# Thirteen seven-product pairs per layer in place of eleven, and a third weight sum made by an accumulating DMA

## The chip, the cores and the metric

The kernel runs on one core of one Trainium2 chip. The metric is the device time of one execution in microseconds (us), taken as the median of several runs. The engines are TensorE (PE, with its weight loads as PEld), VectorE (DVE), ScalarE (ACT), GpSimd (POOL) and SyncE (SP); POOL and SP here mostly issue transfers to the DMA engines.

## The reference, cut to what matters

The model has two layers over 512 tokens of width 1024, all in float32. Each layer has four token mixers and then a gated feed-forward part (FFN) of width 2816 with a causal convolution of three taps. The change touches the FFN's first projection alone:

```python
hf = rms_norm(x, norm_ffn_pre[l])
u = causal_depthwise_conv(hf @ ffn_w_up[l], ffn_conv_w[l], ffn_conv_b[l])
gate, val = jnp.split(u, 2, axis=-1)
f = (jax.nn.gelu(gate, approximate=True) * val) @ ffn_w_down[l]
x = x + rms_norm(f, norm_ffn_post[l])
```

## The kernel before

A float32 product is made of three matmuls of a faster type: each operand is split into a high part (`whi`, a copy by ACT) and the rest (`wlo`, a subtraction by DVE), and high by high, high by low and low by high are summed in PSUM (`mm`, L306). The normalized tokens stand in `hT_hi` and `hT_lo`.

The 2 × 2816 columns of the projection are 22 pairs of 128 gate columns and 128 value columns. Pairs 0 and 1 come in `head`, the others in the loop at the end of the FFN code, in one of two ways. A **plain** pair is two calls of `proj`, 48 matmuls of 512 columns into the tiles `ps`. A pair in the set `SEVEN` (L81) is a **seven pair**: its 2 × 2 block product (two halves of the inner dimension, gate and value columns by two halves of the tokens) is made from seven block products in place of eight, by sums of token blocks (t1 to t4, made once per layer and half by `forms`) and sums of weight blocks (s1 to s4). Its 84 matmuls have 256 columns each and go into the tiles `sa`, `sb` and `se`.

`seven(i)` issues its products in this order: (0,0), then d4 of the pair before; (1,0); d2, whose weights are s2; then (1,1) of the pair before, whose weights are s4; d1 with s1; d3 with s3. All of (0,0), d2, d3 and d4 accumulate in the same bank `sa`, so between them ACT copies partial sums out: L1410 after (0,0), L1418 after d2, L1424 after d3. A copy must be done before the next product adds into the bank.

The weights of a seven pair come as follows. SP loads the first half of the inner dimension as one tile `raw` of 128x1024 (L177), and three slots `rs` of 128x512: L170 (to be s1), L171 (to be s3) and L172 (a block as it is). POOL then adds to two of them by accumulating DMAs: L173 (s1) and L174 (s3). DVE makes s2 from s1 and the first half of `raw` (L206) and s4 from s2 and its other half (L207), and `halves` splits all of them into `whi` and `wlo` (L188, L189). For a plain pair the splits are L245 and L246.

There are three `raw` tiles, four tiles each of `whi` and `wlo`, and 60 slots of 128x512 (`rs`, `s2`, `s4`, `fu` and others). SP's order of instructions is the order in which the code is written, since `MANUAL` holds SP; PE's order in the FFN is written by hand too. The order of ACT, DVE and POOL is set by a scheduler before the program runs; each engine then goes through its instructions in that order, and waits where one of them must wait.

Of the kernel before, what the change touches and what calls it, by code (L numbers as in the profile page):

```python
# [12 lines left out]
ALU = mybir.AluOpType  # L13
# [8 lines left out]
NP_ = DFF // 128  # L22
# [14 lines left out]
def unit_width(k):  # L37
    if k[0] == "fs" and k[2] >= 2:
        return 0
    return {"vt": 816, "w2": 640, "pw": 512, "up": 512}.get(k[0], 1024)  # L40
# [37 lines left out]
SLACK2 = 1.5  # L78
MAXB = 1.5

SEVEN = {i for i in range(5, NP_ - 1) if i % 3 != 1}  # L81

H_2 = 1.0
H_T = 3.0
# [21 lines left out]
def build(tc, x, wts, prm, gains, cst, out, order=None):  # L106
# [4 lines left out]
    V, A, G, T, SP = nc.vector, nc.scalar, nc.gpsimd, nc.tensor, nc.sync  # L111
    with ExitStack() as ctx:
# [10 lines left out]
        def nm(s):  # L123
            uid[0] += 1
            return f"{s}{uid[0]}"

        def slot(w=512, dt=F32, name="g"):
            return pg.tile([128, w], dt, tag="g", bufs=NG, name=nm(name))
# [10 lines left out]
        def dram(src, offset, ap):  # L139
            return src if recording else bass.AP(tensor=src.tensor, offset=src.offset + offset, ap=ap)  # L140
# [8 lines left out]
        raw, parts = {}, {}  # L149
# [9 lines left out]
        def w_dma():  # L159
            while pos["dma"] < len(order) and sum(not isinstance(r, list) for r in raw.values()) < NRAW:  # L160
                i = pos["dma"]
                w = unit_width(order[i][1])
                key = order[i][1]
                if key[0] == "fs" and key[2] == 1:
                    raw[i] = [slot(name="rs") for _ in range(3)]
                    a22, s1, s3 = raw[i]
                    blk = lambda j, c: dram(wts, offs[j] + c, [[1024, 128], [1, 512]])
                    j = i - 1
                    assert order[j][1] == ("fs", key[1], 0)
                    SP.dma_start(s1, blk(i, 512))  # L170
                    SP.dma_start(s3, blk(j, 0))  # L171
                    SP.dma_start(a22, blk(i, 512))  # L172
                    G.dma_start(s1, blk(i, 0), accum_op=ALU.add)  # L173
                    G.dma_start(s3, blk(i, 0), accum_op=ALU.add)  # L174
                elif i not in raw and w:
                    raw[i] = pw.tile([128, WMAX], F32, tag="raw", bufs=NRAW, name=nm("raw"))
                    SP.dma_start(raw[i][:, :w], dram(wts, offs[i], [[w, 128], [1, w]]))  # L177
                pos["dma"] += 1
# [3 lines left out]
        def halves(i, *srcs):  # L182

            hi = pw.tile([128, WMAX], F32R, tag="whi", bufs=NSPL, name=nm("whi"))
            lo = pw.tile([128, WMAX], F32R, tag="wlo", bufs=NSPL, name=nm("wlo"))
            c = 0
            for s, n in srcs:
                A.activation(hi[:, c:c + n], s, AF.Copy)  # L188
                V.tensor_tensor(lo[:, c:c + n], s, f(hi[:, c:c + n]), op=ALU.subtract)  # L189
                c += n  # L190
            parts[i] = (hi, lo)

        def w_seven(i):

            _, p, n = order[i][1]
            if n == 0:
                halves(i, (raw[i], 1024))
                sums[p] = [raw[i], i]  # L200
            elif n == 1:
                r1 = sums[p][0]
                raw.pop(sums[p][1])
                a22, s1, s3 = raw.pop(i)
                s2, s4 = slot(name="s2"), slot(name="s4")
                V.tensor_tensor(s2, s1, r1[:, 0:512], op=ALU.add)  # L206
                V.tensor_tensor(s4, s2, r1[:, 512:1024], op=ALU.add)  # L207
                halves(i, (s2, 512), (s1, 512))
                sums[p] = [s3, a22, s4]
            elif n == 2:  # L210
                halves(i, (sums[p][0], 512), (sums[p][1], 512))
            else:
                halves(i, (sums.pop(p)[2], 512))

        def w_split(q, roomy=False):
# [3 lines left out]
            while pos["spl"] <= min(q, len(order) - 1):  # L219
                i = pos["spl"]  # L220
                w_dma()
                w = unit_width(order[i][1])
                if order[i][1][0] == "fs":
                    w_seven(i)
                    pos["spl"] += 1
                    w_dma()
                    continue
# [12 lines left out]
                else:  # L240
# [6 lines left out]
                    parts[i] = (hi, lo)  # L247
                pos["spl"] += 1
                w_dma()

        def w_ahead(n=NSPL - 1):
# [357 lines left out]
        for l in range(L):  # L609
# [745 lines left out]
            def forms(h):  # L1355
                def block(t, k, q):
                    return f(t[:, k * 4 + h * 2:k * 4 + h * 2 + 2, q * 256:q * 256 + 256])
                hi, lo = (lambda k, q: block(hT_hi, k, q)), (lambda k, q: block(hT_lo, k, q))
                sub, add = ALU.subtract, ALU.add
                a, b = slot(name="ta"), slot(name="tb")  # L1360
                V.tensor_tensor(v2(a), hi(0, 0), hi(0, 1), op=sub)
                V.tensor_tensor(v2(b), lo(0, 0), lo(0, 1), op=sub)
                V.tensor_tensor(a, a, b, op=add)
                form["d1"].append(hilo(a, name="t1"))
                V.scalar_tensor_tensor(v2(b), v2(a), -1.0, hi(1, 1), op0=ALU.mult, op1=sub)
                V.tensor_tensor(v2(b), v2(b), lo(1, 1), op=sub)
                form["d2"].append(hilo(b, name="t2"))
                c = slot(name="tc")
                V.scalar_tensor_tensor(v2(c), v2(b), -1.0, hi(0, 0), op0=ALU.mult, op1=sub)
                V.tensor_tensor(v2(c), v2(c), lo(0, 0), op=sub)  # L1370
                form["d3"].append(hilo(c, name="t3"))
                d = slot(name="td")
                V.scalar_tensor_tensor(v2(d), v2(b), -1.0, hi(1, 0), op0=ALU.mult, op1=sub)
                V.tensor_tensor(v2(d), v2(d), lo(1, 0), op=sub)
                form["d4"].append(hilo(d, name="t4"))
# [24 lines left out]
            def seven(i):  # L1400

                ba, bb, be = bank("sa"), bank("sb"), bank("se")
                sa, sb = slot(name="ca"), slot(name="cb")
                L_, R_ = slice(0, 256), slice(256, 512)
                w0 = w_get(l, ("fs", i, 0))
                w_ahead(1)
                product(ba, w0, 0, (0, 0), True)
                A.activation(sa[:, L_], ba[:, L_], AF.Copy)  # L1410
                w_ahead(2)
                more()
                product(bb, w0, 512, (1, 0), True)
                V.tensor_tensor(bb[:, L_], bb[:, L_], sa[:, L_], op=ALU.add)
                w1 = w_get(l, ("fs", i, 1))
                w_ahead(2)
                product(ba, w1, 0, "d2", False)
                A.activation(sa[:, R_], ba[:, L_], AF.Copy)  # L1418
                w_ahead()
                more()  # L1420
                product(be, w1, 512, "d1", True)
                w2 = w_get(l, ("fs", i, 2))
                product(ba, w2, 0, "d3", False)
                A.activation(sb[:, L_], ba[:, L_], AF.Copy)  # L1424
                w_ahead()

                def four():
                    product(ba, w2, 512, "d4", False)
                    V.tensor_tensor(ba[:, R_], be[:, L_], sb[:, L_], op=ALU.add)

                def three():
                    w3 = w_get(l, ("fs", i, 3))
                    product(be, w3, 0, (1, 1), False)
                    V.tensor_tensor(bb[:, R_], be[:, L_], sa[:, R_], op=ALU.add)
                    ffn_pair(i, [bb, ba], -1.0)
                rest.extend((four, three))

            forms(0)
            for i in range(2, NP_):
                if i == 3:  # L1440
                    forms(1)
                if i in SEVEN:
                    seven(i)
# [147 lines left out]
```

## Time and profile before

| | us |
|---|---|
| median of 3 runs | 1893.99 (1893.16 to 1894.71) |
| the profiled execution | 1895.84 |
| its span from first to last instruction | 1894.1 |
| PE busy | 1873.2 (99%) |
| DVE busy | 1411.3 (75%) |
| ACT busy | 964.0 (51%) |
| POOL busy | 177.2 (9%) |

Busy times are sums over the span of the profiled execution; issuing a DMA isn't counted as busy. The granted clock of TensorE is 1.00 throughout. The FFN pairs of layer 0 lie between about 596 and 820 us, those of layer 1 in the last quarter of the span.

### The profile page before, as it was taken

To read this page: it belongs to the slowest core of one execution; us is meant where nothing else is said; L and a number is where in the kernel's file an instruction comes from. 1 tells how busy PE (TensorE), PEld (TensorE's weight loads), DVE (VectorE), ACT (ScalarE), POOL (GpSimd) and SP (SyncE) were. 2 spreads that over 40 slices of the span, in tenths; PEclk is the share of its full clock that TensorE was granted. 3 is DMA by queue.
4 is the path that set the end of the run, shared out by engine and by line. 5 is a ranking of instruction groups with operands and counts; after the bars stand their busy time and mean duration, and the time that the engine had idled before them with its cause. 6 is when DMAs were issued, how large, how long until landed. Compare 5 with 4: busy or idle time off the path is not lost.

```text
span 1894.1 us, 27567 instructions
## 1 busy us (share of the span) xinstructions
PE 1873.2 (99%) x10164; PEld 1614.9 (85%) x10164; DVE 1411.3 (75%) x2610; ACT 964.0 (51%) x1850; POOL 177.2 (9%) x313
## 2 busy tenths in 40 slices
PE   7999999999999999999999999999999999999998
PEld 7988888888888899988898888888888898999887
DVE  6898879888547888783468887897985478888722
ACT  5547576732435555562345665766224345555521
POOL 0403300000001010100023033000000010110000
PEclk9999999999999999999999999999999999999999
DMA  8523321223245365543454243112232453554332
GB/s 295 153 90 99 104 60 51 67 89 95 86 127 196 105 180 137 147 126 124 159 197 141 67 106 106 57 50 79 89 95 90 146 196 110 156 162 119 122 115 89
DMA packets 87367, 226.41 MB, mean 120 GB/s; under 512 B 12480, under 2 KB 12864, under 8 KB 87232
## 3 DMA queue, kind: packets, MB, share of 16 engines
q1 hardware_dynamic: 73728, 198.42, 32.5%
q0 software_dynamic: 13504, 26.23, 6.9%
q8 instruction: 80, 1.31, 0.3%
q14 instruction: 55, 0.45, 0.1%
HBM read 201.53 MB, written 8.39 MB: 111 GB/s over the span
## 4 chain that ended last, share of the span: by engine, by line
PE 94%; DVE 2%; issue 1%; ACT 1%; DMA 1%; POOL 0%; SPq 0%; DVEq 0%; POOLq 0%; ACTq 0%
PE ps L306 51%; PE tk L306 16%; PE sa L306 6%; PE hd L306 5%; PE o L306 3%; PE se L306 3%; PE vt L306 2%; PE sb L306 2%; PE sB L306 1%; PE sA L306 1%; PE tr L395 1%; PE tB L1086 1%; PE tA L1086 1%; PE cmp L306 1%; PE tA L1185 0%
## 5 line engine op out<-in xcount | busy, mean ns | idle before, releaser
L245 ACT ACTIVATE whi<-raw 128x1024 fp32r<-128x1024 f32 (+2 forms) x274 | 259.0, 949 | 477.7 <-PE ps L306 260.7
L246 DVE TENSOR_TENSOR wlo<-raw,whi 128x1024 fp32r<-128x1024 f32 (+2 forms) x274 | 295.9, 1084 | 232.1 <-ACT whi L245 230.5
L306 PE MATMUL ps<-hT_hi,whi 128*128 128x512 f32 x1136 | 450.2, 396 | 0.8 <-DVE ob L1105 0.8
L306 PE MATMUL ps<-hT_hi,wlo 128*128 128x512 f32 x1136 | 447.7, 394 | 0.0
L306 PE MATMUL ps<-hT_lo,whi 128*128 128x512 f32 x1136 | 446.1, 393 | 0.0
L306 PEld LDWEIGHTS ps<-hT_hi,wlo 128*128 128x128 f32 x1136 | 213.6, 188 | 47.9
L306 PEld LDWEIGHTS ps<-hT_hi,whi 128*128 128x128 f32 x1136 | 213.9, 188 | 44.8 <-DVE ob L1105 1.7
L306 PEld LDWEIGHTS ps<-hT_lo,whi 128*128 128x128 f32 x1136 | 213.9, 188 | 43.9
L908 DVE SCALAR_TENSOR_TENSOR acc<-ct,prm,acc 128x511 f32<-128x511 f32 (+14 forms) x240 | 175.6, 732 | 3.4
L306 PE MATMUL tk<-whi,fh 128*128 128x512 f32 x336 | 130.9, 390 | 0.0
L306 PE MATMUL tk<-wlo,fh 128*128 128x512 f32 x336 | 130.7, 389 | 0.0
L306 PE MATMUL tk<-whi,fl 128*128 128x512 f32 x336 | 130.7, 389 | 0.0
L1065 ACT ACTIVATE P<-P,sm 128x256 f32<-128x256 f32 (+3 forms) x128 | 70.6, 554 | 29.8 <-DVE sm L1063 28.0
L361 POOL TENSOR_TENSOR sm<-sm,mhalf 128x1 f32<-128x1 f32 x32 | 22.1, 690 | 573.1 <-DVE sm L360 573.1
L306 PEld LDWEIGHTS tk<-whi,fl 128*128 128x128 f32 x336 | 63.1, 188 | 13.2
L306 PEld LDWEIGHTS tk<-wlo,fh 128*128 128x128 f32 x336 | 63.1, 188 | 13.0
L306 PEld LDWEIGHTS tk<-whi,fh 128*128 128x128 f32 x336 | 63.1, 188 | 13.0
L306 PE MATMUL hd<-hT_hi,bh 128*128 128x256 f32 x256 | 63.4, 285 | 0.0
L306 PE MATMUL hd<-hT_hi,bl 128*128 128x256 f32 x256 | 62.4, 282 | 0.0
L188 ACT ACTIVATE whi<-rs 128x512 fp32r<-128x512 f32 x66 | 39.2, 627 | 37.5 <-PE ps L306 20.6
L1041 ACT ACTIVATE P<-P,sm 128x512 f32<-128x512 f32 (+1 forms) x80 | 47.2, 629 | 12.6 <-DVE sm L1073 9.7
L189 DVE TENSOR_TENSOR wlo<-rs,whi 128x512 fp32r<-128x512 f32 x66 | 44.3, 684 | 10.7 <-ACT whi L188 10.4
(356 smaller groups left out, 4303.4 us busy)
## 6 DMA issues: line engine op xcount, KB each, us to landing
raw<-wts SPq DMA_DIRECT2D x238, 512.0 KB, 3.5
raw<-wts SPq DMA_DIRECT2D x66, 256.0 KB, 2.6
rs<-wts SPq DMA_DIRECT2D x66, 256.0 KB, 5.2
rs<-wts POOLq DMA_DIRECT2D x44, 256.0 KB, 5.6
br<-wts SPq DMA_DIRECT2D x40, 256.0 KB, 6.1
xr<-x SPq DMA_DIRECT2D x16, 256.0 KB, 5.1
gain<-gains SPq DMA_DIRECT2D x16, 256.0 KB, 5.6
Q<-hlh POOLq DMA_DIRECT2D x64, 64.0 KB, 2.9
```

Source lines behind the costliest of these rows:

```text
L188: A.activation(hi[:, c:c + n], s, AF.Copy)
L189: V.tensor_tensor(lo[:, c:c + n], s, f(hi[:, c:c + n]), op=ALU.subtract)
L245: A.activation(hi[:, c:c + n], s, AF.Copy)
L246: V.tensor_tensor(lo[:, c:c + n], s, f(hi[:, c:c + n]), op=ALU.subtract)
L306: T.matmul(o, lhsT=lhsT, rhs=rhs, start=start, stop=stop, **kw)
L361: G.tensor_tensor(v[:, 1:2], v[:, 0:1], mhalf[:, 0:1], op=ALU.pow)
L395: T.transpose(bs[t, h][:, k * 128:k * 128 + 128], y[h][:, k * 128:k * 128 + 128], ident)
L908: V.scalar_tensor_tensor(acc[i][:, k:], ct[i][:, :512 - k], w[:, 30 - k:31 - k], acc[i][:, k:], op0=ALU.mult, op1=ALU.add)
L1041: A.activation(p, p, AF.Copy, scale=r)
L1065: A.activation(P[i], P[i], AF.Exp, bias=mn[:, i:i + 1], scale=-1.0, accum_out=sm[:, i:i + 1])
L1086: T.transpose(B[j][:, (i - j) * 128:(i - j) * 128 + 128], P[i][:, j * 128:j * 128 + 128], ident)
```

## The change

The set `SEVEN` had the pairs 5, 6, 8, 9, 11, 12, 14, 15, 17, 18 and 20 of each layer; it now has 5 to 7, 9 to 11, 13 to 15 and 17 to 20, that is, 13 in place of 11. Runs of two seven pairs with a plain pair behind them become runs of three, and of four at the end. The sum s2, which DVE made (L206), is now made by DMA: SP loads the first half of `raw`'s columns once more, into a fourth slot (`L171` after the change), and POOL adds s1 to it by a DMA from SBUF to SBUF (L176), which must wait until s1 itself has been summed. DVE still makes s4 (now L208). Behind the changed lines numbers are higher by one, L188 and L189 are now L190 and L191.

```diff
-SEVEN = {i for i in range(5, NP_ - 1) if i % 3 != 1}
+SEVEN = {i for i in range(5, NP_ - 1) if i not in (8, 12, 16)}
...
-                    raw[i] = [slot(name="rs") for _ in range(3)]
-                    a22, s1, s3 = raw[i]
+                    raw[i] = [slot(name="rs") for _ in range(4)]
+                    a22, s1, s3, s2 = raw[i]
...
                     SP.dma_start(s1, blk(i, 512))
+                    SP.dma_start(s2, blk(j, 0))
                     SP.dma_start(s3, blk(j, 0))
                     SP.dma_start(a22, blk(i, 512))
                     G.dma_start(s1, blk(i, 0), accum_op=ALU.add)
                     G.dma_start(s3, blk(i, 0), accum_op=ALU.add)
+                    G.dma_start(s2, s1, accum_op=ALU.add)
...
-                a22, s1, s3 = raw.pop(i)
-                s2, s4 = slot(name="s2"), slot(name="s4")
-                V.tensor_tensor(s2, s1, r1[:, 0:512], op=ALU.add)
+                a22, s1, s3, s2 = raw.pop(i)
+                s4 = slot(name="s4")
                 V.tensor_tensor(s4, s2, r1[:, 512:1024], op=ALU.add)
```

In the programs as built, PE has 10311 matmuls in place of 10167, all differences lie in the FFN parts of the two layers, and the order of the other parts is the same. Three places show what moves.

POOL, in layer 0, the adds for pairs 11, 12 and 14 before (`rs1477` and `rs1478` are s1 and s3 of pair 11, and so on):

```order
L173 DMA rs1477_7164<-wts 128x512
L174 DMA rs1478_7165<-wts 128x512
L173 DMA rs1487_7230<-wts 128x512
L174 DMA rs1488_7231<-wts 128x512
L173 DMA rs1529_7514<-wts 128x512
```

and after, for pairs 13, 14 and 15, a run of three (`rs1521`, `rs1532` and `rs1546` are s2):

```order
L174 DMA rs1519_7448<-wts 128x512
L175 DMA rs1520_7449<-wts 128x512
L176 DMA rs1521_7450<-rs1519_7448 128x512
L174 DMA rs1530_7517<-wts 128x512
L175 DMA rs1531_7518<-wts 128x512
L176 DMA rs1532_7519<-rs1530_7517 128x512
L174 DMA rs1544_7619<-wts 128x512
L175 DMA rs1545_7620<-wts 128x512
L176 DMA rs1546_7621<-rs1544_7619 128x512
```

Each pair's L176 now stands between its own adds and those of the next pair.

ACT, around the copies of the first pair of a run out of its bank, before (`ca1508` and `cb1509` take the copies of pair 11; `rs1487` is s1 of pair 12, `s21512` its s2):

```order
L1410 ACTIVATE ca1508_7360<-sa1505_7357 128x256
L188 ACTIVATE whi1514_7409<-rs1487_7230 128x512
L1418 ACTIVATE ca1508_7360<-sa1505_7357 128x256
L188 ACTIVATE whi1514_7409<-s21512_7405 128x512
L188 ACTIVATE whi1517_7442<-s41497_7321 128x512
```

and after (`ca1555` and `cb1556` take the copies of pair 13; `rs1532` is s2 and `rs1530` s1 of pair 14):

```order
L1411 ACTIVATE ca1555_7659<-sa1552_7656 128x256
L1339 ACTIVATE fu1550_7646<-fu1550_7646 128x512
L190 ACTIVATE whi1560_7706<-rs1532_7519 128x512
L190 ACTIVATE whi1560_7706<-rs1530_7517 128x512
L1419 ACTIVATE ca1555_7659<-sa1552_7656 128x256
L190 ACTIVATE whi1563_7739<-s41540_7610 128x512
L1425 ACTIVATE cb1556_7660<-sa1552_7656 128x256
```

The split of the next pair's s2 has moved from behind the copy L1418 to ahead of it (now L1419).

DVE, at the same place before, where L206 makes s2 of pair 12 and `raw1479` is the other operand:

```order
L189 TENSOR_TENSOR wlo1511_7389<-raw1479_7171,whi1510_7388 128x1024
L206 TENSOR_TENSOR s21512_7405<-rs1487_7230,raw1479_7171 128x512
L1336 SCALAR_TENSOR_TENSOR fu1504_7348<-ps1495_7304,prm19_119,fu1504_7348 128x511
L1336 SCALAR_TENSOR_TENSOR fu1503_7347<-ps1490_7239,prm19_119,fu1503_7347 128x510
L1414 TENSOR_TENSOR sb1506_7358<-sb1506_7358,ca1508_7360 128x256
```

and after, where L208 makes s4 of pair 14 from its s2:

```order
L191 TENSOR_TENSOR wlo1558_7688<-raw1522_7458,whi1557_7687 128x1024
L208 TENSOR_TENSOR s41559_7704<-rs1532_7519,raw1522_7458 128x512
L1337 SCALAR_TENSOR_TENSOR fu1551_7647<-ps1539_7594,prm19_119,fu1551_7647 128x511
L1340 TENSOR_TENSOR fu1538_7585<-fu1537_7584,fu1538_7585 128x512
L1415 TENSOR_TENSOR sb1553_7657<-sb1553_7657,ca1555_7659 128x256
```

The sum s4 stands where s2 was made before, ahead of L1415.

## Rows read from the trace of the kernel before

**Rows 1.** The chain that ended last, by engine, from the profile's page.

```profile
PE 94%; DVE 2%; issue 1%; ACT 1%; DMA 1%; POOL 0%; SPq 0%; DVEq 0%; POOLq 0%; ACTq 0%
```

**Rows 2.** PE's waits, 596 to 820 us: us in total, times, longest.

```profile
PE sa L306 <- ACT cb L1424: 0.3, 1, 0.3
```

**Rows 3.** Busy time by engine in the stretch with the seven pairs of layer 0.

```profile
core 0: us, PE busy (x) PEld busy (x) DVE busy (x) ACT busy (x) POOL busy (x), PEclk, DMA share, GB/s
...
653.70:817.00 163.30, 163.04 (x1144) 152.42 (x1143) 137.44 (x210) 95.69 (x154) 15.89 (x18) 1.00 0.53 143
```

**Rows 4.** The timeline of PE, layer 0, where pairs and products begin: start, length, operation.

```profile
620.74 0.40 PE L306 MATMUL ps<-hT_hi,whi 128*128 128x512 f32 x1
...
653.71 0.28 PE L306 MATMUL sa<-hT_hi,whi 128*128 128x256 f32 x1
...
655.12 0.28 PE L306 MATMUL sb<-hT_hi,whi 128*128 128x256 f32 x1
...
692.02 0.28 PE L306 MATMUL sa<-t3h,whi 128*128 128x256 f32 x1
692.14 0.28 PE L306 MATMUL sa<-t3l,whi 128*128 128x256 f32 x1
...
692.38 0.28 PE L306 MATMUL sa<-hT_hi,whi 128*128 128x256 f32 x1
...
702.40 0.40 PE L306 MATMUL ps<-hT_hi,whi 128*128 128x512 f32 x1
...
723.40 0.28 PE L306 MATMUL sa<-hT_hi,whi 128*128 128x256 f32 x1
```

**Rows 5.** DVE's groups by line and shape: busy us, mean ns, idle before.

```profile
L246 DVE TENSOR_TENSOR wlo<-raw,whi 128x1024 fp32r<-128x1024 f32 x198 | 241.5, 1222 | 210.7 <-ACT whi L245 209.6
L189 DVE TENSOR_TENSOR wlo<-rs,whi 128x512 fp32r<-128x512 f32 x66 | 44.3, 684 | 10.7 <-ACT whi L188 10.4
L189 DVE TENSOR_TENSOR wlo<-raw,whi 128x1024 fp32r<-128x1024 f32 x22 | 26.8, 1220 | 5.4 <-ACT whi L188 4.3 <-DMA raw<-wts 1.1
L206 DVE TENSOR_TENSOR s<-rs,raw 128x512 f32<-128x512 f32 x22 | 15.0, 682 | 0.0
```

**Rows 6.** The DMA view, 640 to 820 us: queue, packets, MB, share of 16 engines.

```profile
q1 hardware_dynamic: 7154, 19.02, 32.8%
q0 software_dynamic: 2674, 4.85, 16.9%
```

**Rows 7.** Timelines of SP and POOL, loads for pair 12, adds for pairs 11 and 12.

```profile
699.13 0.33 SPq L177 DMA_DIRECT2D raw<-wts  x1
699.52 0.49 SPq L170 DMA_DIRECT2D rs<-wts  x1
...
697.33 0.87 POOL L173 DMA_DIRECT2D rs<-wts  x1 [19.54 <-DVE wlo L189]
699.32 0.87 POOL L174 DMA_DIRECT2D rs<-wts  x1 [1.12 <-DVE wlo L246]
708.04 0.87 POOL L173 DMA_DIRECT2D rs<-wts  x1 [7.85 <-DMA rs<-wts]
```

**Rows 8.** Single POOL issues of rows 7, in that order: KB, us from issue to landing.

```profile
rs<-wts POOLq DMA_DIRECT2D x1, 256.0 KB, 4.1
...
rs<-wts POOLq DMA_DIRECT2D x1, 256.0 KB, 7.7
...
rs<-wts POOLq DMA_DIRECT2D x1, 256.0 KB, 4.3
```

**Rows 9.** Timelines of ACT and DVE around pair 11's copy L1418, layer 0.

```profile
719.17 0.64 ACT L188 ACTIVATE whi<-rs 128x512 fp32r<-128x512 f32 x1 [0.84 <-PE sb L306]
...
720.72 0.38 ACT L1418 ACTIVATE ca<-sa 128x256 f32<-128x256 f32 x1 [0.92 <-PE sa L306]
...
721.47 0.42 DVE L1414 TENSOR_TENSOR sb<-sb,ca 128x256 f32<-128x256 f32 x1
```

## The prediction

> **What bounds the kernel now.** I read the chain of waits first: TensorE (PE) holds 94% of it [rows 1]. Next, because a share over the whole program says little about one stage, I read the stage that the change touches, the feed-forward (FFN) pairs of layer 0, from 596 to 820 us. PE's waits there come to one, of 0.3 us [rows 2], and over the stretch with the seven pairs PE is busy for 163.04 of 163.30 us at full clock, VectorE (DVE) for 84%, ScalarE (ACT) for 59%, the DMA engines for 53% [rows 3]. So the stage is PE's: fewer PE microseconds shorten it as long as nothing else becomes late, and nothing else in it is worth time by itself.
>
> The price of a pair is read from where the first matmul of each stands [rows 4]. Pairs 2 to 4 are plain: from 620.74 to 653.71 are 32.97 us, 10.99 for each. Pair 9, the second of a run, takes from 692.38 to 702.40: 10.02 for a seven pair. The stretch from 692.38 to 723.40 holds one plain and two seven pairs: 31.02 − 2 × 10.02 = 10.98 for the plain one, which agrees.
>
> **The change part by part.** *Matmuls.* Pairs 8, 14, 17 and so on change places, but the count is what matters: 13 seven pairs per layer in place of 11, so four pairs in two layers go from 48 matmuls of 512 columns to 84 of 256 (144 matmuls more, as the order has it). Each saves 10.98 − 10.02 = 0.96 us, together **−3.84 us**, all of it on the path. Beside this row the Trainium skill, "TensorE: Matmul & The Clock Gate", section "Back-to-back issue gap", gives an isolated spacing of N/2.4 + 2.5 ns, by which a pair would cost 10.36 and 9.17 us and the change would give 4.74 us (1889.2); by the same section such figures don't hold in a stream, the rows give 0.229 us for 512 columns (10.99/48) where it has 0.216, and I go by the rows.
>
> *DVE.* Gone are 22 sums L206 at 0.68: −15.0. A pair that is converted loses two splits of 1.22 and gains one of 1.22, five of 0.68, the sum s4 (the shape of L206, 0.68) and three sums of 128x256 at 0.42 [rows 5, 9]: 3.40 + 0.68 + 1.26 − 1.22 = 4.12, times four 16.5. Net +1.5 us on an engine that idles 16% of the stretch [rows 3]: nothing on the path. The cover is PE's time: 84% of 31.02 is 26.1 us of DVE; without two L206 24.7, which is three FFN tails F, 2.44 for the plain pair and 6.56 for each seven pair, so F = 3.05 and a seven pair 9.6. A third one beside them makes 34.3 of 41.04, again 84%. Uncovered it would cost at most the 1.5.
>
> *ACT* gains, per converted pair, five splits of 0.64 and three copies of 0.38 [rows 9], at most 4.3, in all 17 us against 41% idle [rows 3]. Nothing, by the same cover; at most a hand-over late by tenths (below).
>
> *GpSimd (POOL).* 26 new DMAs from SBUF into SBUF (L176) and eight more of the old two kinds. Their issuing lasts 0.87 in the rows [rows 7], and POOL stood idle 7.85 us ahead of one [rows 7], so the issue time is free. What isn't free is that L176 must wait until the sum s1 has landed, and that the next pair's L174 and L175 stand behind it on POOL.
>
> *SP and the DMA engines.* One load of 256 KB more per seven pair, at SP's place between s1 and s3. In 640 to 820 us, 19.02 MB by SP took 32.8% of the engines' time and 4.85 MB by POOL 16.9% [rows 6]. Over 180 us that is 0.81 us of all 16 engines for 256 KB loaded and 1.65 for 256 KB added. A run of three seven pairs and a plain one, 41.04 us long, then needs three times 0.81 × 6 (512 KB into raw, four times 256 KB into rs) and 1.65 × 3, and for the plain pair 0.81 × 4: 14.6 + 14.9 + 3.2 = 32.7, about 80%. The same count for before gives 17.9 of 31.02, 58%, where the row has 53% [rows 3]. Still under the bound, but transfers will lie on each other more often, which is what decides their latency.
>
> *How late the new sum is.* No row shows an accumulating DMA whose source is SBUF. Bounds are the landings of the two that add from HBM: 4.1 and 4.3 us when nothing lay beside them, 7.7 with loads beside it [rows 8]; below nothing it can't go, since s2 is needed and was never waited for. The Trainium skill, "DMA: Bandwidth & Descriptors", section "Anatomy of one DMA — SWDGE (gpsimd) path", has about 2.0 us + bytes/436e3, 2.6 us for 256 KB; both additions would then be done by 713.4 and no rival about s2 would stand; the rows are at 4.1 to 7.7, so I keep to the rows.
>
> The tightest pair is the second of a run of three. In the clock of the trace before, pair 12 stands in its place: raw issued at 699.13, the load of s1 at 699.52, the add into s1 at 708.04, eight microseconds later because the loads crowd each other [rows 7]. The add into s1 lands 4.3 to 7.7 later, at 712.3 to 715.7; the add into s2 0.1 after that, to land 4.3 to 7.7 later, at 716.7 to 723.5. I take 7.7 for the first (the third pair's loads now lie beside it, as loads lay beside the 7.7 row) and 4.3 for the second (nothing is issued by SP in between): 708.04 + 7.7 + 0.1 + 4.3 = **720.1**.
>
> When is it needed? PE itself needs s2 only in the next pair. But ACT works in its order: the splits of s2 and s1 of pair 14 stand ahead of the copy L1419 of pair 13, without which PE can't begin the d3 product of pair 13. Before, one split of s1 stood there, at 719.17, and the copy ran at 720.72 [rows 9]. The d3 product, of 12 matmuls at 0.12 [rows 4], ends the pair at 723.40 and so starts at 721.96; the copy must start by 721.5, two splits before it at 0.64 less overlap, so s2 must be there by **720.3**. By my choice it is, by 0.2 us. That is thin, and it is the main risk. Queued behind on POOL are the third pair's adds: issued from 715.9, their s1 lands by 723.6, its s2 at 728.0, and is needed 10.02 later than the second's, at 730.3, so there is more room there. The first pair of a run has its loads issued a plain pair earlier and has more still.
>
> Sum: 1895.84 − 3.84 = 1892.00 for an execution like the profiled one (span 1894.1, with 1.7 around it). The profiled one is 1.85 above the median of the runs, 1893.99, against which the kernel is timed: 1893.99 − 3.84 = **1890.15**.
>
> **The rivals.** *s2 late (ends on the other side).* If the add into s2 lands x after 720.3, ACT stands, the copy with it, and PE with both: x per run with a second pair of this kind, three per layer (pairs 10, 14, 18), six in all; the run 5 to 7 starts long before and has room. For it speak the range up to 723.5 and the 80%; against it that POOL and the queue have until then only these transfers. Price 6x − 3.84: the gain is gone at x = 0.64, slower by over 0.2% from 1.27 on. The late half of the range has a mean of 1.6: 9.6 − 3.84 = +5.8, **1899.8**; its end, 3.2, gives 1909.3.
>
> *Hand-overs.* PE's one wait of 0.3 us was on an ACT copy [rows 2]. With the splits bunched before that copy in every run, once in each of eight runs, 8 × 0.26 ≈ 2 us of the gain goes: **1892.2**, no change that can be told.
>
> *More gain.* Within a seven pair, products on the normalized tokens run faster than on their sums: 12 matmuls between 653.71 and 655.12 took 1.41 [rows 4], where the mean of the pair is 10.02/7 = 1.43. If converted pairs went throughout at 1.41, 9.87 per pair, the saving is 1.11 × 4 = 4.44: **1889.55**. Against it: the same tiles from the same code. The isolated spacing of the clock gate page of the Trainium skill, cited above, would go further that way, to 1889.2.
>
> *The change doesn't do what it says*: the order of instructions has 144 more matmuls, 26 more adds and no L206, and everything outside the FFN stays in place, so this is out.
>
> **How the numbers follow.** A measurement of this kernel can tell about 0.2%, 3.79 us, from no change, and the forecast of −3.84 stands just at that bound. Clean forecast: 0.57, of which it falls past the bound in 0.33 and short of it in 0.24. Late s2: 0.32, of which 0.17 stay within the bound (x under 1.27) and 0.15 beyond. Hand-overs: 0.05, within. More gain: 0.06, faster. Together faster 0.39, same 0.17 + 0.24 + 0.05 = 0.46, slower 0.15. The range goes from 1889.0 (just past the 1889.55 of more gain) to 1898.5, which takes in x up to 1.39 ((1898.5 − 1890.15)/6) and leaves out some 0.13 above; the forecast's own range is 1889.5 to 1892.
>
> **What would show it.** Right: a run of three and its plain pair take 41.04 us from first matmul to first matmul, PE has no waits in the stage, DMA's share there is about 0.8, and the adds L176 land in 4 to 8 us. Wrong: PE waits on ACT's copy L1419 in pairs 9, 13 and 17, with ACT's L190 ahead of it waiting for a DMA into rs and DVE's L208 beside it; then the landing of L176 gives x. If the copy is punctual and the period is still over 41.04, the seven pair's own price was wrong; if PE waits on DVE instead, its cover was.

## The result and the profile after

The changed kernel takes 1917.09 us, the median of six executions, where the kernel before, run beside it, takes 1894.68: slower by 22.4 us. The ratio of the mean times is 1.0125 (95% interval 1.0103 to 1.0147). The forecast was 1890.15, its range ended at 1898.5. One execution of the changed kernel (2640 us) and one of the kernel with an extra reading by ACT below (2066 us) ran at a much lower clock and are left out of the ratios; the median of the other five here is 1916.56.

The profiled execution took 1916.55 us with a span of 1914.8, 20.7 more than before. The page's busy times and its chain, to be held against the table and [rows 1]:

```profile
PE 1874.7 (98%) x10308; PEld 1622.9 (85%) x10308; DVE 1411.5 (74%) x2620; ACT 973.3 (51%) x1878; POOL 206.9 (11%) x347
...
PE 86%; DMA 4%; DVE 3%; issue 3%; ACT 2%; POOL 1%; SPq 0%; DVEq 0%; POOLq 0%; ACTq 0%
```

PE has the 144 matmuls more. Its share of the chain has fallen from 94% to 86%: DMA has gained 3 points, issuing 2, DVE, ACT and POOL one each. What PE waits for, over the whole program (us in total, times, longest), answers to [rows 2]:

```profile
PE sa L307 <- ACT ca L1411: 18.5, 8, 3.7
```

Eight waits, one in the first pair of each run of seven pairs, at the first matmul of the product d2. PE waits for the copy L1411 that takes the product (0,0) out of the bank. For pair 9 the rows of PE (start, length, operation, idle time before it) read, beside [rows 4]:

```profile
694.90 0.28 PE L307 MATMUL sa<-hT_hi,whi 128*128 128x256 f32 x1
...
701.51 0.38 PE L307 MATMUL sa<-t2h,whi 128*128 128x256 f32 x1 [3.73 <-ACT ca L1411]
...
741.40 0.28 PE L307 MATMUL sa<-hT_hi,whi 128*128 128x256 f32 x1
```

From pair 9 to pair 13 are 46.50 us where 41.04 were forecast. Of the 5.46 too many, 3.73 are this wait. ACT's timeline shows why the copy is late; it answers to [rows 9]:

```profile
685.26 1.06 ACT L190 ACTIVATE whi<-raw 128x1024 fp32r<-128x1024 f32 x1 [2.92 <-PE sa L307]
693.73 2.20 ACT L190 ACTIVATE whi<-rs 128x512 fp32r<-128x512 f32 x4 [7.41 <-DMA rs<-rs]
696.07 0.78 ACT L1334 ACTIVATE fu<-sb,prm 128x512 f32<-128x512 f32 x1
696.75 0.77 ACT L1334 ACTIVATE fu<-sa,nb,prm 128x512 f32<-128x512 f32 x1
697.41 0.78 ACT L1334 ACTIVATE fu<-ps,prm 128x512 f32<-128x512 f32 x1
698.07 1.06 ACT L190 ACTIVATE whi<-raw 128x1024 fp32r<-128x1024 f32 x1
699.02 0.78 ACT L1334 ACTIVATE fu<-ps,prm 128x512 f32<-128x512 f32 x1
700.55 0.63 ACT L1339 ACTIVATE fu<-fu 128x512 f32<-128x512 f32 x1 [0.75 <-DVE fu L1337]
701.09 0.36 ACT L1411 ACTIVATE ca<-sa 128x256 f32<-128x256 f32 x1
```

At 686.3, before pair 9 has begun, ACT reaches the split of its s2 and stands for 7.41 us until the sum has landed (the four splits from 693.73 on begin with s2). The split itself is still in time for PE: s2 is split on ACT by 694.4, and PE wants it at 697.8. But all that ACT would have done meanwhile is now queued behind it: with the splits these are ten instructions, which take from 693.7 to 701.1, and the copy stands behind them. Its input was ready at about 696.4, when the product (0,0) ended. Over the program ACT stands six times at such a split:

```profile
ACT whi L190 <- DMA rs<-rs: 38.5, 6, 7.4
```

Why s2 is late is in the rows of SP and POOL, to be read beside [rows 7]. The first list has the loads of s1 for pairs 9, 10 and 11; the second POOL's adds for pair 9 (s1, s3 and s2) and the one into s2 of pair 10; the third what the adds of 678.77 and 687.01 took to land (KB, us). The release that the profile names at 678.77 is inferred; the load of s1 landed at 678.2.

```profile
673.10 0.91 SPq L170 DMA_DIRECT2D rs<-wts  x1
...
678.15 0.42 SPq L170 DMA_DIRECT2D rs<-wts  x1
...
683.80 0.50 SPq L170 DMA_DIRECT2D rs<-wts  x1
```

```profile
678.77 0.88 POOL L174 DMA_DIRECT2D rs<-wts  x1 [32.81 <-ACT whi L190]
680.20 0.87 POOL L175 DMA_DIRECT2D rs<-wts  x1 [0.56 <-PE se L307]
687.01 0.87 POOL L176 DMA_DIRECT2D rs<-rs  x1 [5.93 <-DMA rs<-wts]
...
695.42 0.87 POOL L176 DMA_DIRECT2D rs<-rs  x1 [5.74 <-DMA rs<-wts]
```

```profile
rs<-wts POOLq DMA_DIRECT2D x1, 256.0 KB, 8.0
...
rs<-rs POOLq DMA_DIRECT2D x1, 256.0 KB, 6.6
```

The weights of all three pairs of a run are loaded in one burst, from 673 to 686. Load, sum and sum of the first pair stand one behind the other in it: 5.7 us to the issue of the first add, 8.0 until it has landed, 6.6 for the second, together 20.6 us with the small gaps between, and ACT's place for the result is 13.2 us after the load's issue. The window rows of that stretch show the crowding, which the experiments below take up, and a second cost (the columns are those of [rows 3]):

```profile
672.00:684.00 12.00, 12.00 (x92) 11.47 (x91) 11.19 (x18) 7.50 (x12) 1.75 (x2) 1.00 0.78 235
684.00:708.00 24.00, 20.27 (x126) 18.54 (x125) 15.26 (x24) 10.87 (x18) 6.20 (x7) 0.93 0.92 223
...
700.00:702.00 2.00, 0.49 (x4) 0.49 (x5) 2.00 (x4) 0.90 (x2) 0.26 (x1) 1.00 1.07 311
702.00:704.00 2.00, 2.00 (x14) 2.00 (x13) 2.00 (x3) 1.86 (x4) 0.87 (x1) 0.62 0.79 152
704.00:706.00 2.00, 2.00 (x12) 2.00 (x12) 2.00 (x5) 0.10 (x1) 0.00 (x0) 0.53 0.91 186
706.00:710.00 4.00, 4.00 (x36) 4.00 (x35) 2.16 (x4) 1.40 (x3) 0.00 (x0) 1.00 0.34 103
```

The DMA engines are busy for 92% of the 24 us in which the sums are made. And after the wait PE's granted clock is near 0.5, the lower of its two levels (1.2 GHz), until 706: 2 × 0.38 + 2 × 0.47 = 1.7 us more. With 3.73 that is 5.4, the whole excess of this run.

Over the program: 18.5 us of waits, less 0.3 before; three of the eight waits (3.73, 2.80 and 2.64 us long) were followed by such a stretch of 3.4 us, which began within the wait in two of the cases and cost 1.5 to 1.7 us each, 4.8 together; and −3.84 from the matmuls. That makes 19.2 of the 20.7 us between the two spans.

### The profile page after: what moved, and what is told of

Same layout as the page of the kernel before. It is cut to its first block, busy times and chain, and to the rows that moved or that the text cites. A ratio compares the mean times of both kernels' runs of the same rounds, so it can differ in the third digit from the quotient of the medians.

```text
span 1914.8 us, 28046 instructions
## 1 busy us (share of the span) xinstructions
PE 1874.7 (98%) x10308; PEld 1622.9 (85%) x10308; DVE 1411.5 (74%) x2620; ACT 973.3 (51%) x1878; POOL 206.9 (11%) x347
## 4 chain that ended last, share of the span: by engine, by line
PE 86%; DMA 4%; DVE 3%; issue 3%; ACT 2%; POOL 1%; SPq 0%; DVEq 0%; POOLq 0%; ACTq 0%
PE ps L307 45%; PE tk L307 16%; PE sa L307 6%; PE hd L307 5%; PE o L307 3%; PE se L307 3%; DMA rs<-rs 2%; PE vt L307 2%; DMA rs<-wts 1%; PE sB L307 1%; PE sA L307 1%; PE tr L396 1%; PE sb L307 1%; DVE fu L1337 1%; PE tB L1087 1%
## 5 line engine op out<-in xcount | busy, mean ns | idle before, releaser
L246 ACT ACTIVATE whi<-raw 128x1024 fp32r<-128x1024 f32 (+2 forms) x266 | 250.5, 946 | 473.3 <-PE ps L307 266.6
L247 DVE TENSOR_TENSOR wlo<-raw,whi 128x1024 fp32r<-128x1024 f32 (+2 forms) x266 | 286.2, 1080 | 229.4 <-ACT whi L246 224.1
L307 PE MATMUL ps<-hT_hi,whi 128*128 128x512 f32 x1072 | 424.8, 396 | 0.8 <-DVE ob L1106 0.8
L307 PE MATMUL ps<-hT_hi,wlo 128*128 128x512 f32 x1072 | 422.4, 394 | 0.0
L307 PE MATMUL ps<-hT_lo,whi 128*128 128x512 f32 x1072 | 421.0, 393 | 0.0
L307 PEld LDWEIGHTS ps<-hT_hi,wlo 128*128 128x128 f32 x1072 | 201.6, 188 | 45.2
L307 PEld LDWEIGHTS ps<-hT_hi,whi 128*128 128x128 f32 x1072 | 201.8, 188 | 42.7 <-DVE ob L1106 1.7
L307 PEld LDWEIGHTS ps<-hT_lo,whi 128*128 128x128 f32 x1072 | 201.8, 188 | 41.7
L191 DVE TENSOR_TENSOR wlo<-rs,whi 128x512 fp32r<-128x512 f32 x104 | 68.4, 686 | 39.8 <-ACT whi L190 38.2
L190 ACT ACTIVATE whi<-rs 128x512 fp32r<-128x512 f32 x104 | 59.4, 622 | 71.3 <-DMA rs<-rs 38.5
L307 PEld LDWEIGHTS tk<-whi,fl 128*128 128x128 f32 x336 | 63.1, 188 | 13.2
```

The source lines that it names most:

```text
L307: T.matmul(o, lhsT=lhsT, rhs=rhs, start=start, stop=stop, **kw)
```

## The experiments

**What makes s2.** Three kernels differ from the change in how s2 is made or in how many pairs there are. The first is the kernel before with the new set of pairs:

```diff
-SEVEN = {i for i in range(5, NP_ - 1) if i % 3 != 1}
+SEVEN = {i for i in range(5, NP_ - 1) if i not in (8, 12, 16)}
```

> The thirteen seven pairs per layer of the change, with s2 made by DVE as before (three slots, no third sum by DMA). Theory A (the time is lost because ACT stands at the split of the first pair's s2, which the DMA sum brings late, and the copy L1411 behind it is late): no such stand here, so the gain of the matmuls appears, 1890 to 1892 us, with PE waits on L1411 under 3 us in all. Rival B (runs of three are too dense for DVE and ACT whatever makes s2): DVE has 0.68 us more per pair than after the change, PE waits of 15 us or more remain, 1908 to 1920 us.

Measured: 1890.94 us against 1894.42, ratio 0.9982 (0.9972 to 0.9991), −3.5 us. PE waits 0.27 us in each layer, and a run's period is 41.04 us to the hundredth:

```profile
694.96 0.28 PE L306 MATMUL sa<-hT_hi,whi 128*128 128x256 f32 x1
...
736.00 0.28 PE L306 MATMUL sa<-hT_hi,whi 128*128 128x256 f32 x1
```

So runs of three are not too dense, and rival B falls: the whole loss, and 26 us between this kernel and the change, hangs on the DMA sum. At the place where ACT stands in the change, its rows here read as follows; s2 is the `s` split at 691.46, and the copy L1410 is on time:

```profile
685.32 1.06 ACT L188 ACTIVATE whi<-raw 128x1024 fp32r<-128x1024 f32 x1 [0.66 <-PE sa L306]
688.01 0.63 ACT L188 ACTIVATE whi<-rs 128x512 fp32r<-128x512 f32 x1 [1.63 <-PE ps L306]
...
691.46 0.63 ACT L188 ACTIVATE whi<-s 128x512 fp32r<-128x512 f32 x1
...
696.56 0.37 ACT L1410 ACTIVATE ca<-sa 128x256 f32<-128x256 f32 x1
```

So the scheduler has not left ACT's order as it was: in the change the split of s2 comes first behind that of raw, 5.1 us earlier than here. By an estimate from these rows, a sum that lands at 693.65 would keep ACT standing for some 2 us at the place of this kernel, and the other 5 of the 7.4 us come from the earlier place. No run separates the two.

The second kernel is the change with the old set of eleven pairs:

```diff
-SEVEN = {i for i in range(5, NP_ - 1) if i not in (8, 12, 16)}
+SEVEN = {i for i in range(5, NP_ - 1) if i % 3 != 1}
```

> The eleven pairs and runs of two of before, with s2 by the accumulating DMA from SBUF. Theory A: the chain of two sums is late in every run whose loads come in a burst, but a burst of two pairs is shorter; ACT stands 1 to 4 us at the split of s2 and PE waits 0 to 1.5 us in each of eight or ten runs: 1894 to 1906 us. Theory A2 (only the burst of three pairs makes it late): 1893 to 1895 us and no PE wait on L1411.

Measured: 1900.61 us, ratio 1.0034 (1.0020 to 1.0047). PE's waits:

```profile
PE sa L307 <- ACT ca L1411: 5.2, 4, 1.8
```

The four places are the first pair (5) of each layer, 1.04 us each, and pair 8, 1.81 and 1.31. A burst of two is enough, then, but only in the second run of a layer; the later runs of two go without a wait. The time lies in the range of theory A, but the waits are not those that it gave, in eight or ten runs.

**Which pair.** In two kernels s2 is made by DMA in some pairs and by DVE (the old L206) in the others: by DVE in the first pair of each run alone, and by DMA there alone.

```diff
-                    SP.dma_start(s2, blk(j, 0))
+                    if key[1] - 1 in SEVEN:
+                        SP.dma_start(s2, blk(j, 0))
...
-                    G.dma_start(s2, s1, accum_op=ALU.add)
+                    if key[1] - 1 in SEVEN:
+                        G.dma_start(s2, s1, accum_op=ALU.add)
...
+                if not (p - 1 in SEVEN):
+                    V.tensor_tensor(s2, s1, r1[:, 0:512], op=ALU.add)
```

> The change, but s2 of the first pair of each run (5, 9, 13, 17) is made by DVE, the others' by DMA. Theory A: the first pair's s2 is the late one, so the stands of ACT at a DMA go and with them PE's waits, 1890 to 1893 us. Rival (the second pair's s2 is the late one, as the prediction had it, or the crowding of the DMA engines itself): PE's waits stay, over 1905 us.

Measured: 1895.30 us, ratio 1.0003 (0.9994 to 1.0013); the profiled execution took 1893.47. The waits on the first pair's copy are gone, those of the first runs too. What is left is the place that the prediction had named, small. PE waits for the copy behind d2 (L1423 here, L1419 of the change):

```profile
PE sa L311 <- ACT ca L1423: 1.9, 2, 1.2
```

ACT stands 0.90, 3.06 and 3.50 us at the s2 of a second pair, and PE waits 0.75 and 1.19 us in the last run of each layer. Slower than expected by 2 us or more; the waits of the profiled execution explain its 1.7 us over that of the kernel with DVE sums (1891.74), the spread of the others (1892 to 1898) is not explained.

With the condition reversed (`not in SEVEN`):

> The reverse: only the first pair of each run has its s2 by DMA, the others by DVE. Theory A: as slow as the change, 1910 to 1918 us, ACT standing 5 to 7 us at six splits of s2; fewer transfers may make each a little shorter (two additions less in the burst, 3 us of DMA time). Rival (second pair): under 1895 us.

Measured: 1923.09 us, ratio 1.0140 (1.0120 to 1.0161); one of the four executions took 1914.68. ACT's waits, and PE's in the same eight places (L1415 is L1411 of the change):

```profile
ACT whi L192 <- DMA rs<-rs: 40.0, 6, 7.7
```

```profile
PE sa L311 <- ACT ca L1415: 20.0, 8, 4.0
```

The first pair alone makes the whole loss. Eight sums by DMA in place of 26, and 18 loads fewer, leave the first pair's chain as late as it was. The time is past the expected 1918: behind four of the waits the granted clock fell, which cost PE 10.5 us where it cost 4.8 in the change.

**Dependence or crowding.** The third load and the DMA sum are made, but nothing reads them; DVE makes an s2 of its own:

```diff
-                a22, s1, s3, s2 = raw.pop(i)
-                s4 = slot(name="s4")
+                a22, s1, s3, s2 = raw.pop(i)
+                s2, s4 = slot(name="s2"), slot(name="s4")
+                V.tensor_tensor(s2, s1, r1[:, 0:512], op=ALU.add)
```

> Thirteen pairs; the third load and the DMA sum are made as in the change, but nothing reads them: s2 is made by DVE as before. Theory A (the dependence of ACT on the late sum costs the time): 1890 to 1893 us, PE waits on ACT's copies under 3 us in all. Rival B2 (the transfers themselves, or POOL's standing at L176 ahead of the next pair's sums, make s1 and s3 late too): PE waits of 5 us or more, over 1897 us.

Measured: 1892.06 us, ratio 0.9988 (0.9979 to 0.9998). PE's one wait in the pairs:

```profile
PE sa L308 <- ACT cb L1426: 0.3, 1, 0.3
```

The transfers, and POOL's standing at L176 ahead of the next pair's adds, cost little: 1.1 us lie between this and 1890.94, 1.4 when each is taken against the kernel before beside it, and the two intervals overlap. And this although loads into rs now took a median of 8.4 us in the FFN of layer 0.

Then the same kernel, in which ACT reads one column of the unread sum in the first pair of each run, at the place where the change splits it. No operand of PE depends on it:

```diff
+                if p - 1 not in SEVEN:
+                    A.activation(small(1, name="touch"), sd[:, 0:1], AF.Identity, bias=f(touch.pop(p)[:, 0:1]))
                 halves(i, (s2, 512), (s1, 512))
```

(`sd` is the DMA sum; the bias is a column of the pair's split raw, which puts the reading behind that split.)

> The run with the unread DMA sum once more (s2 by DVE), but in the first pair of each run ACT reads one column of the DMA sum, where the change has it split: behind the split of raw and ahead of the other splits and of the copy L1411. Nothing that PE uses depends on it. Theory A (head of line on ACT): ACT stands 5 to 7 us there in six runs, the copy of the first pair is late, PE waits for it 1.5 to 4 us per run, 10 to 22 us in all, 1903 to 1920 us. Rival D (PE waits in the change because its own operands, s2's parts, are late): 1890 to 1894 us, as with the unread sum.

Measured: 1934.81 us, the median of three executions, ratio 1.0213 (1.0196 to 1.0230). ACT's and PE's waits, and the first of them in ACT's timeline:

```profile
ACT touch L213 <- DMA rs<-rs: 46.8, 6, 9.5
```

```profile
PE sa L312 <- ACT ca L1416: 28.6, 6, 6.4
```

```profile
695.22 0.29 ACT L213 ACTIVATE touch<-rs,whi 128x1 f32<-128x1 f32 x1 [8.87 <-DMA rs<-rs]
```

An instruction of 0.29 us whose result nobody uses costs 43 us. Rival D falls: PE waits because ACT stands, whatever ACT stands for. It stands longer here than in the change (7.8 to 9.5 us at three places of layer 0), PE's waits are longer (3.1 to 6.4), and each of the six was followed by a stretch at the lower clock; that it went past the expected 1920 is of this kind.

**What makes the sum late.** The sum over 32 of its 512 columns only; the rest of that addition is left out:

```diff
-                    G.dma_start(s2, s1, accum_op=ALU.add)
+                    G.dma_start(s2[:, 0:32], s1[:, 0:32], accum_op=ALU.add)
```

> The change with the sum s1 into s2 over 32 of the 512 columns alone (the rest of that addition is left out). Theory A, where the lateness is that of the bytes of two sums one behind the other: L176 lands 2 to 3 us after its issue in place of 5 to 7, ACT stands 2 to 4 us at the first pair's s2 in place of 5.5 to 7.4, PE's waits on L1411 fall from 18.5 us to 2 to 8, 1892 to 1901 us. Rival (a small one waits behind the queue as long as a large one): landings stay over 5 us, over 1908 us.

Measured: 1907.2 us in two executions (1904.67 and 1909.72), ratio 1.0070 (1.0050 to 1.0090), in the range of neither case. PE's waits:

```profile
PE sa L307 <- ACT ca L1411: 12.7, 8, 2.0
```

The sixteenth part of the bytes lands a median of 3.1 us after its issue in place of 5.0 (640 to 820 us), but where it matters, at the first pair, hardly earlier (single issues at 678.96 and 686.59, KB and us):

```profile
rs<-wts POOLq DMA_DIRECT2D x1, 256.0 KB, 7.4
...
rs<-rs POOLq DMA_DIRECT2D x1, 16.0 KB, 6.0
```

16 KB took 6.0 us where 256 KB had taken 6.6. At all six first pairs in question it is 5.5 to 6.9 us in place of 6.6 to 8.2. The next 16 KB, of pair 10, landed in 2.1 us; the windows of the two (columns as in [rows 3]) differ in the DMA engines' share, 1.09 and 0.34:

```profile
686.59:692.60 6.01, 6.01 (x34) 5.14 (x33) 1.49 (x2) 0.78 (x1) 2.65 (x3) 1.00 1.09 339
694.73:696.85 2.12, 2.12 (x15) 1.87 (x14) 2.12 (x5) 1.98 (x4) 1.77 (x2) 1.00 0.34 38
```

So the lateness of the second sum is mostly waiting beside other transfers, not its own bytes, and two thirds of the chain, 13.9 of 20.6 us in the change, lie ahead of it. The Trainium skill, "DMA: Bandwidth & Descriptors", section "Issuing engines are not separate DMA queues", has it that transfers started by any of the engines run on the same 16 DMA engines and interleave; these rows agree, with POOL's 16 KB beside SP's loads. By that page's section "Anatomy of one DMA — SWDGE (gpsimd) path" 256 KB would be estimated at 2.6 us; measured here were 5.0 in the median and 6.6 where it mattered.

**Earlier loads, another order.** Four raw tiles in place of three, and 58 slots in place of 60, so that loads are issued earlier:

```diff
-NG = 60
-NRAW = 3
+NG = 58
+NRAW = 4
```

> The change with four raw tiles in place of three (and 58 slots in place of 60), so that the loads of a run's first pair are issued some 5 to 11 us earlier. Theory A (the chain load, sum, sum takes about 20 us from the release of a raw tile and ends after ACT's place for it): s2 lands before or within 2 us of ACT's place, PE waits on L1411 under 4 us in all, 1890 to 1896 us. Rival (the burst only moves, with ACT's places, or PE's waits come from ACT's own load): PE waits over 10 us, over 1903 us.

Measured: 1916.7 us, ratio 1.0120 (1.0100 to 1.0140). In the six runs in question ACT now stands three times, for 2.1 to 2.6 us, and PE not at all: earlier loads do cure them. But the time is 20 us past the expected. With the other pools the scheduler found another order elsewhere: PE waits 4.07 us in the first run of each layer, where ACT stands at no DMA, with 4.1 us lost to the lower clock behind these waits, and some 8 us more in the mixers. Some 4 us of the loss lie in none of these. As a version it is no better; for the cause its waits speak for theory A.

ACT's order in the FFN as the code is written:

```diff
-            ffn_order.enter_context(tc.manual_schedule(engines={E_T}))
+            ffn_order.enter_context(tc.manual_schedule(engines={E_T, E_A}))
```

> The change with ACT's order in the FFN as the code is written: the tail of the pair before (two L1334, one L1339) and the next split of raw no longer stand between the split of the first pair's s2 and its copy L1411; two L1334 and one L1339 of the plain pair still do. Theory A (head of line: ACT stands at s2, and what is queued between it and the copy makes PE wait): ACT still stands 4 to 7 us at the DMA, but PE's waits on L1411 fall by about 2 us per run, to 2 to 8 us in all, 1893 to 1903 us, if the new order makes no waits of its own. Rival D (PE waits for the parts of s2 themselves): PE's waits stay at 15 us or more, over 1908 us.

Measured: 1935.05 us, ratio 1.0217 (1.0196 to 1.0237); a failed experiment. ACT stands at a DMA for 0.4 us in all, not 4 to 7 a run, since in this order it comes to s2 later, and yet PE waits 20.8 us on L1411. The waits moved: ACT waits 85.5 us for DVE ahead of the activations L1339 (18.6 in the change), one of which stands ahead of the copy. It can't tell A from D; its waits, too, are for what stands ahead of L1411 on ACT.

**More pairs without the DMA sum.** DVE makes s2; 14 and 16 seven pairs per layer:

```diff
-SEVEN = {i for i in range(5, NP_ - 1) if i % 3 != 1}
+SEVEN = {i for i in range(5, NP_ - 1) if i not in (10, 15)}
```

> 14 seven pairs per layer (all from 5 to 20 but 10 and 15), s2 by DVE, no DMA sum. If PE still bounds: six converted pairs at 0.96 us, -5.8 us, 1888 to 1890 us. If DVE bounds within runs of four and five (9.6 + 0.68 = 10.3 us of DVE for a seven pair against PE's 10.02): PE waits of 0.3 us per pair of a long run, 1890 to 1893 us.

```diff
-SEVEN = {i for i in range(5, NP_ - 1) if i % 3 != 1}
+SEVEN = set(range(5, NP_ - 1))
```

> All 16 pairs from 5 to 20 as seven pairs, s2 by DVE. If PE still bounds: ten converted pairs, -9.6 us, 1884 to 1886 us. If DVE bounds (10.3 us a pair against 10.02, for 16 pairs in each of two layers, 9 us): the gain is given back in large part, 1889 to 1896 us, with DVE over 95% busy in the FFN stretch and PE waits on copies.

Measured: 1889.82 us, ratio 0.9975 (0.9965 to 0.9984), −4.5 us where six pairs at 0.96 make −5.8, and 1884.89 us, ratio 0.9950 (0.9935 to 0.9964), −9.4 us where ten pairs make −9.6. The window row of the FFN of layer 0 with 16 pairs (columns as in [rows 3]):

```profile
653.70:820.00 166.30, 166.05 (x1364) 164.56 (x1363) 158.53 (x257) 110.88 (x193) 22.98 (x26) 1.00 0.63 160
```

DVE is 95% busy and PE still doesn't wait for it. This version is faster than both kernels.

## Why the prediction was wrong, by its own steps

- **Matmuls, −3.84 us: right.** With the sum on DVE the same pairs gave −3.5, the period of a run was the forecast 41.04 us, and ten pairs gave −9.4. The spacing from the rows held. The 4.74 of the isolated figure (its own terms, 10.36 and 9.17, make 4.76) did not come; it is the period that tells the two apart, since the totals are known to some 2 us only.
- **DVE's cover: right, and wider than reckoned.** The sum of rows had a seven pair with L206 at 10.3 us of DVE; the stretch with 16 of them shows 95% busy, some 9.6 a pair: the lengths of DVE's instructions there add up to 176.4 us, but they overlap in part and keep it busy for 158.5.
- **POOL's and SP's added work as such: right.** Unread, it cost 1.1 to 1.4 us. DMA's share over pair 9 to pair 13 was 0.68 of 46.5 us, 31.6 us of work, where 32.7 were reckoned.
- **How late the sum is: right for the pair that was reckoned, too short for the other.** For the second pair of a run it took 7.7 and 4.3 us for the two adds; those of pair 10, issued at 687.59 and 695.42, took (KB, us):

```profile
rs<-wts POOLq DMA_DIRECT2D x1, 256.0 KB, 7.5
...
rs<-rs POOLq DMA_DIRECT2D x1, 256.0 KB, 3.3
```

  Those of pair 9, in the middle of the burst, took 8.0 and 6.6. The range of 4.1 to 7.7 came from three rows; an add of 9.7 us, issued at 668.56, stood in the same trace of before. Nor had the 4.1 and 4.3 "nothing" beside them: loads landed until 699.4 and 710.0, within these adds.
- **The step that failed** is the sentence that the first pair of a run "has its loads issued a plain pair earlier and has more still". It was taken from the loads alone, and even for them the trace of before did not bear it out. There the loads of pair 11, the first of a run, begin 24.2 us before the pair (rows below), those of pair 12 at 699.13 [rows 7], 24.3 us before 723.40 [rows 4]:

```profile
692.14 0.33 SPq L177 DMA_DIRECT2D raw<-wts  x1
```

```profile
716.37 0.28 PE L306 MATMUL sa<-hT_hi,whi 128*128 128x256 f32 x1
```

  In the change the loads of s1 for pairs 9 and 10 are 5.1 us apart (673.10 and 678.15), the pairs themselves 7.0 even without a wait, so the first has the least time of its run. And ACT's place for the first pair's s2 is early, at 686.3, 8.6 us before the pair begins; the chain of load and two adds ends 7.4 us behind it. The prediction had looked for ACT's place in the second pair only, and had weighed s2 by when PE needs it: there it was in time by some 3 us. That ACT, once it stands, takes its whole queue with it was seen for the copy L1419 of that pair, but not asked for every place where a split of s2 stands in ACT's order. The mechanism of the rival was right, at L1411 in place of L1419 and in the first pair in place of the second. Of the second pair only 0.75 and 1.19 us a layer showed, once the first was cured.
- **The price of it was too low.** Six waits of 1.83 to 3.73 us made 16.3 together, where the rival's mean was 9.6; the lower clock behind three of them, 4.8, was not in the prediction at all.
- **Hand-overs: the sum came, by coincidence.** In the first run of each layer (pair 5) ACT stands at no DMA, but has four L1334 in a row ahead of L1411:

```profile
653.38 2.77 ACT L1334 ACTIVATE fu<-ps,prm 128x512 f32<-128x512 f32 x4
...
656.03 0.39 ACT L1411 ACTIVATE ca<-sa 128x256 f32<-128x256 f32 x1
```

  PE waits 1.14 and 1.04 us. The rival's 2 us had been eight waits of 0.26, one in each run. With the sum on DVE the same pairs have two of them there and no such wait, so this, too, came with the DMA sum, through the order that the scheduler gave ACT.

Not settled: why the runs of two in the kernel with eleven pairs stall only in the second run of a layer, and why the kernel with DVE sums in the first pairs alone spreads from 1892 to 1898.

## What to carry to other kernels

A transfer that feeds an engine working in order must be held against that engine's place for it, in every repetition of the pattern, not against the time at which its consumer at the end needs it: one wait puts the whole queue behind it late, and what is last in that queue may be what the bounding engine waits for. Before a sum is moved from an engine with room to the DMA queues, count the chain (load, add, add) in the burst in which it will run, with latencies from crowded rows. And try the larger change without the move: here DVE, which was to be relieved, had room for five pairs more per layer.

## What the runs showed of the hardware

An idle PE cost more than its idle time: behind waits of 3.73, 2.80 and 2.64 us the granted clock lay at 0.5 for 3.4 us in the changed kernel, while after others of 1.83, 2.59 and 2.74 us it stayed at 1.00. With the first pair's sums alone by DMA four of six such waits were followed by it, at a cost of 10.5 us, and that kernel, with less work for the DMA engines, was the slower one. An accumulating DMA of 16 KB from SBUF to SBUF took 6.0 us where the DMA engines' share was 1.09 and 2.1 us where it was 0.34.
